# Output projection of a hybrid decoder layer: turning the normed rows three steps later, and the last weight sum behind a bank's reading

## Chip, cores and metric

The kernel runs on one core of one Trainium2 chip. The metric is the device time of one execution in microseconds (us), the median of several runs. TensorE is called PE here (PEld its weight loads), VectorE DVE, ScalarE ACT, GpSimd POOL, and SyncE, which issues most of the transfers, SP.

## What is computed

One decoder layer on a sequence of 512 rows of 1024 features in float32: a norm, an input projection, three mixing branches (dilated attention, pooling, a state space scan), gates, an output projection with the residual, then a second norm and a feed-forward part. The change lies between the output projection and the first products of the feed-forward part:

```python
merged = gates[:, :, 0] * y_a + gates[:, :, 1] * y_b + gates[:, :, 2] * y_c
x = x + merged @ w_o[i]
x = x + conv_ffn(rmsnorm(x, ln2_g[i]), ffn_w_up[i], ffn_conv_w[i], ffn_conv_b[i], ffn_w_down[i])
```

## The kernel before

Every operand of a product is split into a high part (a cast, `wh` for a weight) and a low part (the rest, `wl`), and a product is three passes: high by high, high by low, low by high. Weights come as jobs. While job n multiplies, `prepare` makes the low part of job n+1 (`low`, one DVE instruction over the tile), casts job n+2 (`cast`, two halves on ACT) and fetches job n+3. A job can have a `form`, which computes its raw weight before the cast. With `spread` the halves of a cast are put on the list `second` and issued one at each later step; with `once`, or where a job is late, they are issued at once. In `cast` the `form` is called first in either case.

The order on the engines is written out by hand: each engine executes its instructions in the order in which the program issues them. `step()` is called between blocks of products. It first flushes one entry of `second` (so one half of a cast), then advances each generator in `running` by one `yield`. `after(n, it)` puts n empty steps before a generator.

The output projection is done in seven products instead of eight (`wo_group`): two, five, three, one, six, seven, four, each with sums of weight quarters and sums of the merged rows. Each product has two blocks, one for each of two row blocks of 128 (tb 0 and 1 or 2 and 3), of 12 matmuls of 128x512. Six, seven and four add onto the banks of one, so a block must wait until the block before it on that bank has been read (`read`, DVE adds the bank to the rows `x`). The weight of four is `total(four.raw, four.raw, W[2])`, one DVE instruction over 128x2048.

After six reads a bank, the rows of tb 0 (then tb 1) are complete in both halves, and `then` norms them: `norm_late` squares them on ACT, takes the square root, and after its first `yield` computes the reciprocal, the factor `rt` and the normed rows `u` (one half on DVE, one on ACT). `norm_turn` transposes `u` on PE (8 transposes), casts the result to `uh` on ACT (2) and subtracts to `ul` on DVE (2). For tb 0 and 1 the generator `rest` was advanced once where it was made, so `u` was computed right behind the reading, and the transposes came two steps later:

```python
if tb < 2:
    r = rest()
    next(r)
    running.append(after(1, r))
```

For tb 2 and 3, which four completes, the remaining part is called from the first products of the up projection (`opening`, line 1531), which multiply the columns of tb 0 and 1 first, and those of tb 2 and 3 later. Two small transposes (`fcol`) of the convolution's constants stand among the blocks too.

Of the kernel before, what the change touches and what calls it, by code (L numbers as in the profile page):

```python
# [71 lines left out]
class Job:  # L72


    def __init__(self, parts, k, c, body):
        self.parts, self.k, self.c, self.body = parts, k, c, body
        self.raw = self.split = None
        self.late = self.short = self.once = False
        self.load = self.form = self.then = None


# [1 line left out]
def trunk(ctx: ExitStack, tc, out, x, rel_bias, ln1_g, w_in, b_gate, w_a, pool_w, pool_scale, w_b,  # L83
# [22 lines left out]
    def T(name, dt=F32, shape=(P, S)):  # L106
        return big.tile(list(shape), dt, name=name, tag="t")
# [7 lines left out]
    def small(name, shape, dt=F32):  # L115
        return tiny.tile(list(shape), dt, name=name, tag="tiny")
# [7 lines left out]
    waiting, running = [], []  # L124
# [38 lines left out]
    def after(n, it):  # L163
        for _ in range(n):
            yield
        yield from it
# [18 lines left out]
    def cast(job, cuts=1, spread=False, other=None):  # L185


        w = job.c // cuts
        if job.form:
            job.raw = job.form()  # L190
        job.high = whp.tile([P, job.k, job.c], F32R, name="wh", tag="wh")

        def high(i):
            o = slice(i * w, (i + 1) * w)
            (other.tensor_copy if other and i else act.copy)(job.high[:, :, o], job.raw[:, :, o])  # L195

        def at(i):
            high(i)
            if i + 1 < cuts:
                second.append(lambda: at(i + 1))  # L200

        if spread:
            second.append(lambda: at(0))
            return
        for i in range(cuts):
            high(i)
# [212 lines left out]
    def rstd_of(ss, cols, n):  # L419

        sq, v, r, t, r2 = (small(nme, [P, cols]) for nme in ("sq", "v", "r", "rt", "r2"))
        dve.tensor_scalar(v, ss, 1.0 / n, EPS, OP.mult, OP.add)
        act.activation(sq, v, AF.Sqrt)
        dve.reciprocal(r, sq)
        if cols == 1:
            dve.scalar_tensor_tensor(t, r, v, r, OP.mult, OP.mult)
        else:
            dve.tensor_mul(t, r, r)
            dve.tensor_mul(t, t, v)
        dve.tensor_scalar(t, t, -0.5, 1.5, OP.mult, OP.add)  # L430
        dve.tensor_mul(r2, t, r)
        return r2
# [14 lines left out]
    def norm_turn(us, uh, ul, tb):  # L447
        for h in range(2):
            ps = SM("uT")
            for j in range(4):  # L450
                pe.transpose(ps[:, j * P:(j + 1) * P], us[h][:, j * P:(j + 1) * P], eye)  # L451
            pv = ps.rearrange("p (j t) -> p j t", j=4)
            hh = uh[:, 4 * h:4 * h + 4, tb * P:(tb + 1) * P]
            act.copy(hh, pv)
            dve.tensor_sub(ul[:, 4 * h:4 * h + 4, tb * P:(tb + 1) * P], pv, hh.bitcast(F32))
# [10 lines left out]
    def norm_late(t, g, v0, outs, last, h=1, apart=False):  # L466


        ss, v, sq, r, rt = (small(n, [P, 1]) for n in ("ss", "v", "sq", "r", "rt"))
        squares(act, t, ss)  # L470
        act.activation(sq, ss, AF.Sqrt, bias=v0, scale=1.0 / D)
        xg = None
        if not apart:
            xg = T("xg")
            dve.tensor_tensor(xg, t, g[h], OP.mult)
        dve.scalar_tensor_tensor(v, ss, -0.5 / D, last, OP.mult, OP.add)
        yield xg

        dve.reciprocal(r, sq)
        dve.scalar_tensor_tensor(rt, r, v, r, OP.mult, OP.mult)  # L480
        dve.scalar_tensor_tensor(rt, rt, 1.5, r, OP.add, OP.mult)

        if apart:
            o1, (o0, x0) = outs()
            dve.scalar_tensor_tensor(o1, t, rt, g[h], OP.mult, OP.mult)
            act.mul(o0, x0, rt)
            return
        (o1, x1), (o0, x0) = outs(xg)
        act.mul(o0, x0, rt)
        dve.tensor_scalar(o1, x1, rt, None, OP.mult)  # L490
# [772 lines left out]
    def wo_group():  # L1263
# [34 lines left out]
        def then(tb, h):  # L1298
            if "uh" not in nxt:
                nxt["uh"] = upool.tile([P, KD, S], F32R, name="uh2", tag="uh")  # L1300
                nxt["ul"] = upool.tile([P, KD, S], F32R, name="ul2", tag="ul")
            v0, vh, xg0 = nxt[tb]
            us = [T("u0"), T("u1")]
            it = norm_late(X1[tb, h], nxt["g2"], v0,
                           lambda: (us[h], (us[1 - h], xg0)), vh, h, True)
            next(it)

            def rest():
                next(it, None)
                yield  # L1310
                norm_turn(us, nxt["uh"], nxt["ul"], tb)

            if tb < 2:
                r = rest()
                next(r)
                running.append(after(1, r))
            elif tb == 2:
                r2 = rest()
                next(r2)
                late.append(r2)  # L1320
            else:
                late.append(rest())
                for _ in late_split.pop(0):
                    pass
# [50 lines left out]
        def total(out, a, b, op=OP.add):  # L1375
            dve.tensor_tensor(out, a, b, op)
            return out
# [3 lines left out]
        three = job(4, None, lambda: W[1], B, (0, 1), more=True)  # L1381
        one = job("A11", quarter(0, 0), None, A, (0, 0), behind=lambda tb, h: first(tb, 1))
        six = job(2, None, lambda: W[2], A, (0, 1), more=True, op=OP.subtract, behind=then)
        seven = job(3, None, lambda: W[1], A, (1, 1), more=True, op=OP.subtract,
                    behind=lambda tb, h: first(tb, 0))
        four = job("A22", quarter(1, 0), lambda: total(four.raw, four.raw, W[2]), A, (1, 0), more=True,
                   behind=then)
        one.then = lambda: total(W[1], W[2], one.raw, OP.subtract)
        four.late, inner = True, four.body

        def body(ws):
# [209 lines left out]
    def program():  # L1601
# [21 lines left out]
        for group, next_ in zip(groups, groups[1:] + (None,)):  # L1623
# [4 lines left out]
            for i, job in enumerate(group.jobs):  # L1628
# [14 lines left out]
        many = {"a": branch_jobs(0, w_a, AO, 3), "g": gate_jobs(2),  # L1643
                "Z": z_jobs(0), "z": z_jobs(1)}
        load, sums, group = wo_group()
        for token in MIX:
            if token == "w":
# [119 lines left out]
    for tb in range(2):  # L1767
        s0, s1, v, sq, r, rt = (small(n, [P, 1]) for n in ("s0", "s1", "v", "sq", "r", "rt"))
# [13 lines left out]
    dve.tensor_copy(g1, first[2][:, :KD])  # L1782

    cast(weights[0], 2, other=dve)
    low(weights[0], 2, pool)
    for k in range(KD):
        turn_scale(1, k % 2 * 4 + k // 2)
    for k in range(KD):
        turned(k, 0, bank(k))
    cast(weights[1], 2)  # L1790
    parts = lows(weights[1], 2)

# [3 lines left out]
    r = rstd_of(ss, 2, D)  # L1796
# [25 lines left out]
    fetch(weights[3])  # L1822
    begin(0, 256, S)
    cast(weights[2])
    low(weights[2])
    begin(1, 256, S)
# [4 lines left out]
    n = 0  # L1831
# [68 lines left out]
```

## Time and profile before

| | us |
|---|---|
| median of 3 runs | 1026.0 |
| lowest, highest | 1025.07, 1026.0 |
| the profiled execution | 1025.94 |
| its span | 1024.2 |

The profile is one execution. The page gives the busy time of each engine, the chain of work that ended last, and groups of instructions by line. Answers of the trace give waits (who waited for whom), the timeline (instructions in order of time, merged where they follow each other) and windows (busy time, granted TensorE clock and DMA in stretches of the span). Times in them are counted from the start of the span. Ends of matmuls are modelled, some 0.16 us behind the next one's start, so starts are compared with starts.

### The profile page before, as it was taken

The page shows a single profiled execution, that of the slowest core. Times are in us where ns is not written, and L with a number is a line of the kernel's source. Part 1 is how long each engine was busy: PE and PEld are TensorE (multiplying, and loading weights), DVE is VectorE, ACT ScalarE, POOL GpSimd, SP SyncE. Part 2 cuts the span into 40 slices and gives each one's busy share as a digit, 9 for nine tenths or more (in the row PEclk, how much of TensorE's full clock was granted, in tenths as well). Part 3 has the DMA queues.
Part 4 walks back from the last instruction along what each step waited for, and adds up shares of the span by engine and source line. Part 5 has one row for each costly group of instructions (what it writes and reads, how often), then busy time and mean ns, then how long its engine had stood idle before and what let it go on. Part 6 is the DMA issues. An engine that isn't in the chain of part 4 may idle for free.

```text
span 1024.2 us, 13621 instructions
## 1 busy us (share of the span) xinstructions
PE 1007.2 (98%) x5378; PEld 858.4 (84%) x5378; DVE 718.8 (70%) x910; ACT 518.8 (51%) x877; POOL 141.3 (14%) x128
## 2 busy tenths in 40 slices
PE   8999999999999999999999999799999999999997
PEld 8998878999988888888888887598888888888885
DVE  6554767687757647667889687658778768685756
ACT  5433545554445476878567235554454434433434
POOL 1681000010000000000064402102111100111002
PEclk9999999999999999999999999899999999999999
DMA  8548312165254353552266255333232232321332
GB/s 255 182 110 200 108 58 79 53 155 179 90 172 107 86 134 96 143 144 83 83 166 187 91 163 149 123 110 98 86 120 83 92 114 79 128 83 42 124 103 83
DMA packets 114624, 121.26 MB, mean 118 GB/s; under 512 B 6500, under 2 KB 96167, under 8 KB 114560
## 3 DMA queue, kind: packets, MB, share of 16 engines
q1 hardware_dynamic: 111087, 114.81, 36.4%
q0 software_dynamic: 2880, 4.72, 2.8%
q8 instruction: 42, 0.69, 0.3%
q10 hardware_dynamic: 592, 0.86, 0.2%
q14 instruction: 23, 0.18, 0.1%
HBM read 116.58 MB, written 3.00 MB: 117 GB/s over the span
## 4 chain that ended last, share of the span: by engine, by line
PE 96%; DVE 2%; ACT 1%; DMA 1%; issue 0%; ACTq 0%; DVEq 0%
PE pa L236 35%; PE pu L236 22%; PE pb L236 11%; PE pd L236 7%; PE pqk L236 6%; PE pq L236 3%; PE pa L1748 2%; PE ps L784 1%; PE pu L1531 1%; PE ppw L236 1%; PE po L832 1%; PE pt L818 1%; PE py L1117 1%; DMA xin<-in_x_dram 1%; PE pyo L1124 1%; PE uT L451 0%
## 5 line engine op out<-in xcount | busy, mean ns | idle before, releaser
L215 DVE TENSOR_TENSOR wl<-raw,wh 128x2048 fp32r<-128x2048 f32 (+3 forms) x87 | 202.8, 2331 | 49.3 <-ACT wh L195 27.9
L195 ACT CAST wh<-raw 128x1024 fp32r<-128x1024 f32 (+4 forms) x171 | 171.6, 1021 | 71.4 <-DVE raw L359 17.8
L1426 DVE SCALAR_TENSOR_TENSOR hc<-pu,fcol,hc 128x510 f32<-128x510 f32 x88 | 65.9, 749 | 56.1 <-ACT hc L1423 54.5
L236 PE MATMUL pa<-uh,wh 128*128 128x512 f32 (+1 forms) x368 | 88.9, 381 | 0.0
L236 PE MATMUL pa<-ul,wh 128*128 128x512 f32 (+1 forms) x368 | 86.8, 375 | 0.0
L236 PE MATMUL pa<-uh,wl 128*128 128x512 f32 (+1 forms) x368 | 86.7, 375 | 0.0
L236 PE MATMUL pu<-uh,wh 128*128 128x512 f32 (+1 forms) x352 | 83.5, 379 | 0.0
L236 PE MATMUL pu<-ul,wh 128*128 128x512 f32 (+1 forms) x352 | 83.5, 379 | 0.0
L236 PE MATMUL pu<-uh,wl 128*128 128x512 f32 (+1 forms) x352 | 83.5, 379 | 0.0
L236 PEld LDWEIGHTS pa<-ul,wh 128*128 128x128 f32 x368 | 66.7, 188 | 12.6
L236 PEld LDWEIGHTS pa<-uh,wl 128*128 128x128 f32 x368 | 66.7, 188 | 12.5
L236 PEld LDWEIGHTS pa<-uh,wh 128*128 128x128 f32 x368 | 65.4, 189 | 11.8
L236 PEld LDWEIGHTS pu<-uh,wl 128*128 128x128 f32 x352 | 64.2, 188 | 12.5
L236 PEld LDWEIGHTS pu<-ul,wh 128*128 128x128 f32 x352 | 64.2, 188 | 12.5
L236 PEld LDWEIGHTS pu<-uh,wh 128*128 128x128 f32 x352 | 64.1, 188 | 12.4
L1423 ACT ACTIVATE hc<-pu,fcol,fcol 128x512 f32<-128x512 f32 x40 | 31.2, 779 | 78.9 <-PE pu L236 78.8
L1431 POOL TENSOR_TENSOR hc<-hc 128x512 f32<-128x512 f32 x22 | 30.8, 1399 | 284.3 <-DVE hc L1426 252.1
L215 DVE TENSOR_TENSOR wl<-w,wh 128x2048 fp32r<-128x2048 f32 (+1 forms) x22 | 47.3, 2151 | 10.2 <-issue 4.6
L806 ACT ACTIVATE sb<-sb,nmls 128x128 f32<-128x128 f32 (+1 forms) x72 | 30.0, 418 | 31.4 <-DVE nmls L803 20.8
L195 ACT CAST wh<-w 128x1024 fp32r<-128x1024 f32 (+1 forms) x44 | 41.0, 972 | 4.8 <-PE pb L236 2.4
L1100 POOL TENSOR_TENSOR st<-st,dts 128x512 f32<-128x512 f32 x4 | 4.2, 1049 | 225.9 <-ACT st L1108 163.9
L1428 ACT ACTIVATE hc<-hc 128x512 f32<-128x512 f32 x22 | 13.9, 632 | 40.2 <-DVE hc L1426 40.1
(424 smaller groups left out, 1948.8 us busy)
## 6 DMA issues: line engine op xcount, KB each, us to landing
raw<-in_w_in_dram SPq DMA_DIRECT2D x24, 1024.0 KB, 5.6
raw<-in_ffn_w_up_dram SPq DMA_DIRECT2D x22, 1024.0 KB, 5.1
raw<-in_ffn_w_down_dram SPq DMA_DIRECT2D x8, 1024.0 KB
raw<-in_w_in_dram SPq DMA_DIRECT2D x14, 512.0 KB, 5.6
raw<-in_w_in_dram SPq DMA_DIRECT2D x8, 768.0 KB
raw<-in_w_b_dram SPq DMA_DIRECT2D x4, 1024.0 KB
al<-ad SPq DMA_DIRECT2D x16, 256.0 KB, 6.2
raw<-in_w_c_dram SPq DMA_DIRECT2D x4, 1024.0 KB, 5.2
```

Of the source, the lines that this page charges most:

```text
L195: (other.tensor_copy if other and i else act.copy)(job.high[:, :, o], job.raw[:, :, o])
L215: (eng or dve).tensor_tensor(l[:, :, o], job.raw[:, :, o], h[:, :, o].bitcast(F32), OP.subtract)
L236: pe.matmul(ps, l, r, start=first and n == 0, stop=last and n == total - 1, skip_group_check=onto)
L784: pe.matmul(pss[i][:, o:o + w * P], q[r, n * P:(n + 1) * P], k[r, kb * P:(kb + w) * P], start=True, stop=True)
L806: act.activation(sb[:, off:off + w * P], sb[:, off:off + w * P], AF.Exp, bias=nm[:, n, h:h + 1], accum_out=ls[:, n, h:h + 1])
L818: pe.transpose(pt[:, o:o + P], sb[:, o:o + P], eye)
L832: pe.matmul(po[DH * hh:DH * hh + DH, n * P:(n + 1) * P], V[g, kb + i][:, (2 * c + hh) * DH:(2 * c + hh + 1) * DH], probs[2 * c + hh, nb][: ...
L1423: act.activation(t, ps, AF.Identity, bias=ff["c1"][:, ff["b"] + m:ff["b"] + m + 1], scale=fw(2, m))
L1426: dve.scalar_tensor_tensor(t[:, sh:], ps[:, :S - sh], fw(k, m), t[:, sh:], OP.mult, OP.add)
L1428: act.activation(t, t, AF.Silu)
L1431: pool.tensor_tensor(a, a, t, OP.mult)
L1748: pe.matmul(first[2 * n + j][:, lo:hi], a[:, k, j * P:(j + 1) * P], b[:, k, lo:hi], start=a is wh and b is uh and k == 0, stop=a is wl and ...
```

## The change

`rest` takes a count of empty steps, and for tb 0 and 1 it goes into `running` without being advanced: the reciprocal, the factor and `u` are computed at the next step, behind the flush of a cast, and the transposes three steps after that. Job four becomes `lazy` and six is no longer `once`: the weight sum of four and the first half of its cast are issued by the flush of the next step, behind the reading of six's first bank and the square on it, and the second half one step later.

```diff
-        self.late = self.short = self.once = False
+        self.late = self.short = self.once = self.lazy = False
...
-        if job.form:
+        if job.form and not (spread and job.lazy):
             job.raw = job.form()
...
         def at(i):
+            if i == 0 and job.lazy:
+                job.raw = job.form()
             high(i)
...
-            def rest():
+            def rest(n=1):
                 next(it, None)
-                yield
+                for _ in range(n):
+                    yield
                 norm_turn(us, nxt["uh"], nxt["ul"], tb)

             if tb < 2:
-                r = rest()
-                next(r)
-                running.append(after(1, r))
+                running.append(rest(3))
...
         one.then = lambda: total(W[1], W[2], one.raw, OP.subtract)
+        six.once, four.lazy = False, True
         four.late, inner = True, four.body
```

## The prediction

> **What bounds the kernel now.** I read the page first: the engines' busy time and the chain that ended last.
>
> ```profile
> span 1024.2 us, 13621 instructions
> ...
> PE 1007.2 (98%) x5378; PEld 858.4 (84%) x5378; DVE 718.8 (70%) x910; ACT 518.8 (51%) x877; POOL 141.3 (14%) x128
> ...
> PE 96%; DVE 2%; ACT 1%; DMA 1%; issue 0%; ACTq 0%; DVEq 0%
> ```
>
> TensorE (PE) is busy for 98% of the span and carries 96% of the chain, so a change pays only where PE stands still or runs slowly. The waits of PE over the whole span come next (waiting line, releaser, us in total, times, longest).
>
> ```profile
> PE uT L451 <- ACT u L486: 6.9, 1, 6.9
> PE uT L1765 <- DVE diag L1777: 2.0, 2, 1.7
> ```
>
> One wait stands out: 6.9 us, once, before the transposes of the normed rows, which the change moves. Windows of the span show what PE does around it (stretch, its length, PE, PEld, DVE, ACT, POOL busy, PEclk, DMA share, GB/s).
>
> ```profile
> 6.00:7.00 1.00, 0.00 (x0) 0.00 (x0) 0.85 (x4) 0.55 (x2) 0.00 (x0) 1.00 1.10 350
> 640.00:642.00 2.00, 2.00 (x11) 1.65 (x10) 2.00 (x1) 0.00 (x0) 0.15 (x1) 1.00 0.00 0
> 644.00:646.00 2.00, 0.00 (x0) 0.00 (x0) 1.10 (x2) 1.39 (x2) 0.00 (x0) 0.91 0.97 347
> 646.00:648.00 2.00, 0.00 (x0) 0.00 (x0) 0.16 (x1) 1.98 (x4) 0.00 (x0) 0.50 1.05 373
> 655.00:656.00 1.00, 1.00 (x4) 0.73 (x3) 1.00 (x2) 1.00 (x2) 0.00 (x0) 0.56 0.00 0
> 690.00:1016.00 326.00, 326.00 (x1444) 270.08 (x1444) 237.03 (x257) 141.51 (x194) 36.79 (x26) 1.00 0.29 95
> ```
>
> From 690 to 1016 PE is busy without a gap at full clock, so what is won before 690 arrives at the end, unless a later load turns late. In the wait the granted clock falls to 0.50 (a mean of 0.91 over 644 to 646 puts the fall at 645.6) and is back only near 655.9 (0.56 over 655 to 656). The timeline shows the wait link by link (start, us, engine, line, operation).
>
> ```profile
> 633.13 0.34 SPq L510 DMA_DIRECT2D fcol1r<-in_ffn_conv_b_dram  x1
> ...
> 639.83 2.47 DVE L215 TENSOR_TENSOR wl<-w,wh 128x2048 fp32r<-128x2048 f32 x1
> ...
> 641.52 1.07 PE L236 MATMUL pb<-wh,sal 128*128 128x512 f32 x4
> ...
> 642.22 2.28 DVE L1376 TENSOR_TENSOR raw<-raw,w 128x2048 f32<-128x2048 f32 x1
> ...
> 642.42 1.07 PE L236 MATMUL pb<-wl,sah 128*128 128x512 f32 x4
> 644.42 0.68 DVE L1350 TENSOR_TENSOR x<-x,pb 128x512 f32<-128x512 f32 x1
> 644.61 1.99 ACT L195 CAST wh<-raw 128x1024 fp32r<-128x1024 f32 x2 [5.07 <-DVE raw L1376]
> 646.50 0.62 ACT L437 ACTIVATE junk<-x 128x512 f32<-128x512 f32 x1
> ...
> 647.25 0.16 DVE L476 SCALAR_TENSOR_TENSOR v<-ss,vo 128x1 f32<-128x1 f32 x1 [2.16 <-ACT junk L437]
> ...
> 648.86 0.16 DVE L479 RECIPROCAL r<-sq 128x1 f32<-128x1 f32 x1 [1.45 <-ACT sq L471]
> ...
> 649.51 0.75 DVE L485 SCALAR_TENSOR_TENSOR u<-x,rt,grow 128x512 f32<-128x512 f32 x1
> 649.57 0.72 ACT L486 ACTIVATE u<-xg,rt 128x512 f32<-128x512 f32 x1 [0.74 <-DVE rt L481]
> 650.17 0.68 DVE L1350 TENSOR_TENSOR x<-x,pb 128x512 f32<-128x512 f32 x1
> ...
> 650.34 1.97 PE L451 MATMUL uT<-eye,u 128*128 128x128 f32 x8 [6.85 <-ACT u L486]
> ...
> 651.96 2.05 PE L236 MATMUL pb<-wh,sbh 128*128 128x512 f32 x4
> ...
> 652.68 0.72 ACT L486 ACTIVATE u<-xg,rt 128x512 f32<-128x512 f32 x1 [0.74 <-DVE rt L481]
> ...
> 656.62 0.27 PE L516 MATMUL fcol0p<-eye,fcol0r 128*128 128x128 f32 x1
> ...
> 657.01 1.09 PE L451 MATMUL uT<-eye,u 128*128 128x128 f32 x8
> ...
> 657.86 1.17 PE L236 MATMUL pb<-wh,sbh 128*128 128x512 f32 x4
> ```
>
> Job six has issued its last matmul at 643.3. Its first bank, done long before, is read only at 644.42, because `wl` of job seven and the weight sum of job four hold VectorE (DVE). The square on it starts at 646.50, because the cast of that sum holds ScalarE (ACT). So u is ready at 650.3, and job seven, which needs no u, stands behind the transposes.
>
> **The old cost.** From 643.3 to 650.34 are 7.0 us of no issue. Then 8 transposes, 12 matmuls of seven and no more take 650.34 to 656.62, 6.3 us. At full clock 8 transposes are 0.85 (657.01 to 657.86), 4 matmuls 0.90 (641.52 to 642.42) and so 12 are 2.7: 3.6 in all. The slow clock cost 2.7 us, the pause 7.0: 9.7 together.
>
> **The change, part by part.** The instructions are the same ones; only their places on PE, DVE and ACT move. By the instruction order of the changed program, PE goes: seven's first block, the two `fcol` transposes, seven's second block, transposes of block 0, four's first block, transposes of block 1, four's second block, then the opening of the up projection. DVE goes: `wl` of seven, first reading, v, weight sum, reciprocal to u, second reading, its chain, `wl` of four, the readings of seven. The second half of four's cast stands behind the second square root. Further durations:
>
> ```profile
> 655.11 2.28 DVE L215 TENSOR_TENSOR wl<-raw,wh 128x2048 fp32r<-128x2048 f32 x1
> ...
> 658.65 1.05 ACT L454 CAST uh<-uT 128x512 fp32r<-128x512 f32 x2
> ...
> 658.78 0.15 DVE L461 TENSOR_SCALAR v<-ss 128x1 f32<-128x1 f32 x1 [0.79 <-ACT junk L437]
> ...
> 659.35 1.28 DVE L455 TENSOR_TENSOR ul<-uT,uh 128x512 fp32r<-128x512 f32 x2
> ...
> 666.14 2.08 PE L1531 MATMUL pu<-uh,wh 128*128 128x256 f32 x16
> ...
> 668.05 2.09 PE L1531 MATMUL pu<-ul,wh 128*128 128x256 f32 x16
> ...
> 668.29 2.29 DVE L215 TENSOR_TENSOR wl<-raw,wh 128x2048 fp32r<-128x2048 f32 x1
> ...
> 679.38 1.12 PE L236 MATMUL pu<-uh,wh 128*128 128x256 f32 x8
> ```
>
> *First stall.* The first reading takes the weight sum's old start, 642.22, and ends at 642.9. Seven's first block follows six at 643.3 unstalled and issues to 646.0, the `fcol` transposes (656.62 to 657.01, 0.4) to 646.4; their data is there, for the last load was issued at 633.13 and DMA carries nothing over 640 to 642. Seven's second block adds onto the bank that the second reading empties. On DVE v comes 0.75 after the square's start (646.50 to 647.25), at 643.7; the weight sum runs 643.8 to 646.0; reciprocal to second reading is 1.31 (648.86 to 650.17), so that reading starts at 647.3 and ends at 648.0. PE waits from 646.4: 1.6 us. The square root needs 2.36 from square to reciprocal (646.50 to 648.86), to 645.3, and is covered by the sum.
>
> *Second stall.* Seven's second block and block 0's transposes (u long ready) issue to 651.6. Four's first block needs the reading of seven's first bank, which stands behind the second chain and `wl` of four. Reading to the end of u is 3.2 us (650.17 to 653.40), so `wl` starts at 650.4 and runs 2.28 to 652.7; cast halves of 1.0 fit before it (646.1 and 649.0). The reading ends at 653.3: PE waits 1.7 us.
>
> *Third stall.* Four's first block, transposes, second block: 2.7 + 0.85 + 2.7, to 659.6. The opening needs `uh` of block 1, whose casts stand on ACT behind the norm of row block 2, and that norm hangs on DVE: v and copies (658.78 to 659.35, 0.6) after the square, to 654.6; reading of seven's second bank 0.7; its square, v and the start of `ul`, 1.3, to 656.6; two `ul` 1.2, to 657.8; reading of four's first bank, whose chain ends with u at 661.0. The first of two casts (0.5 of 1.05) ends at 661.5: PE waits 1.9 us.
>
> *Fourth.* Thirty-two matmuls of 0.12 (16 in 666.14 to 668.05) and transposes issue to 666.3; the `wl` that follows ends at 666.6 (two `ul` to 662.8, reading 0.7, square and v 0.9, `wl` 2.29): 0.4 us.
>
> After that comes the old order: 16 + 32 + 16 matmuls and a set of transposes, 8.5 us from 666.6 to 675.2, against 679.3 (row 679.38; its weight load issues 0.1 ahead). In sum 9.7 less 1.6 + 1.7 + 1.9 + 0.4 is **4.1 us**. The same link lengths, set into the old order, give back 679.3.
>
> Queues: SP's second `w` load waits for the weight sum, 1.5 us later; behind it the next up-projection load waits for `wl` of four, which ends at 652.7 instead of 657.4. So weights come earlier. POOL's order is kept.
>
> *The unknown.* Does PE keep its clock through pauses of 1.6 to 1.9 us? The nearest row is the first window: at 6 to 7 us PE stood in a 1.65 us wait at clock 1.00, and the known fall came 2.1 us after the last matmul (643.5). All three pauses lie below that, and nearer the first, so I take none. The other end is one slow spell: twelve matmuls took 651.96 to 656.62, 4.7 instead of 2.7, so 2.0 us. The Trainium skill, "TensorE: Matmul & The Clock Gate", section "What's actually happening", puts the fall after an idle window of about 3.4 us of a free-running counter. By that no pause here would slow PE, and the sum stays 4.1; the trace's fall after 2.1 us speaks for a shorter one.
>
> **The rivals.** *One slow spell.* Block 0's transposes and the second stall together are 2.6 us without a product, more than 2.1. If transposes do not hold the clock, four's first block runs at half, costing up to 2.0, of which some 0.8 hides in the third stall's DVE chain; a fall in the third stall costs 1.5. Gain 2.1 to 2.9, so about 1023.4. For it: recovery at 655.9 came 5.5 us after the transposes began but 3.9 after the products; against it: only one event. The same page, Part 4, says that transposes do not count as PE activity; its result would be this rival's.
>
> *The clock never recovers: slower.* Recovery took 5.5 us of unbroken issue; the new stalls lie 3.6 and 6 us apart. If the first stall drops the clock and every further one restarts the count, PE runs at half from 648 to 668: 10 us of work in 20, where the forecast does 16 (20 less 4 of stalls). That costs 6: 1.9 us slower than now, 1027.9. It decides from a slow stretch of some 14 us on. Against it: the 1.65 us pause at full clock.
>
> *Nothing left.* DVE now sets three PE restarts in a row. If hand-overs between ACT and DVE each take longer than in the old order, by 2 us over the chain of some 15 links, the gain falls under 0.2%: 1024.5 to 1026. Against it: the link lengths reproduce the old timeline.
>
> **How the numbers follow.** The profiled execution took 1025.94 (span 1024.2 and 1.7 around it); the median is 1026.0, so I subtract from that: 1026.0 − 4.1 = 1021.9, own range 1020.4 to 1023. Chances: forecast 0.62, one spell 0.2, nothing left 0.11, slower 0.07. About 0.2%, 2.05 us, is what measurement can tell: faster below 1023.95. That is the forecast and most of the spell (0.18): 0.8; within 0.13; slower 0.07. The range 1020.4 to 1024.8 takes in the spell at its dearest (1021.9 + 2.0) and part of the third rival.
>
> **What would show it.** Right: PE's 6.9 us wait gone, in its place waits of about 1.6, 1.7 and 1.9 us on `x` L1350 or its line, and on `uh`; full clock over 640 to 670; the opening at 661.5 instead of 666.1; the tail matmuls at 675.2 instead of 679.4. Wrong: a clock of 0.50 anywhere from 646 to 668, a stall above 2.5 us, a wait after 690, or the tail later than 677.

## The result, and the profile after

| | before | after |
|---|---|---|
| median of 7 runs each, us | 1025.58 | 1021.8 |
| lowest, highest, us | 1024.67, 1026.0 | 1021.59, 1022.39 |
| the profiled execution, us | 1025.94 | 1021.8 |
| its span, us | 1024.2 | 1020.0 |

The ratio of the times is 0.9967, 95% interval 0.9955 to 0.9979: faster, by 4.1 us in the profiled executions and 3.8 between the medians, where 4.1 was forecast.

The waits of PE in the changed kernel (waiting line, releaser, us in total, times, longest; lines stand one or two lower than before):

```profile
PE pb L238 <- DVE x L1351: 3.0, 2, 1.5
PE pu L1533 <- ACT uh L456: 1.5, 1, 1.5
...
PE pb L238 <- DVE wl L217: 0.2, 1, 0.2
```

The wait of 6.9 us on `u` is gone; two waits on the readings of banks and one on `uh` stand in its place. The timeline of PE says where they are (start, us, operation, in brackets the idle time before and its releaser):

```profile
642.46 1.07 PE L238 MATMUL pb<-wl,sah 128*128 128x512 f32 x4
...
648.04 1.21 PE L238 MATMUL pb<-wh,sbh 128*128 128x512 f32 x4 [1.49 <-DVE x L1351]
...
650.94 1.03 PE L453 MATMUL uT<-eye,u 128*128 128x128 f32 x8
653.45 1.17 PE L238 MATMUL pb<-wh,mgh 128*128 128x512 f32 x4 [1.47 <-DVE x L1351]
...
661.56 2.18 PE L1533 MATMUL pu<-uh,wh 128*128 128x256 f32 x16 [1.49 <-ACT uh L456]
...
665.50 1.03 PE L453 MATMUL uT<-eye,u 128*128 128x128 f32 x8
666.63 2.18 PE L1533 MATMUL pu<-uh,wl 128*128 128x256 f32 x16
...
675.26 1.12 PE L238 MATMUL pu<-uh,wh 128*128 128x256 f32 x8
```

From the last matmul group of job six (row 642.46, before 642.42) to the first group of the tail (675.26, before 679.38) PE needs 32.80 us instead of 36.96: 4.16 less, the whole gain. On DVE and SP the same stretch shows the links that set these starts:

```profile
642.25 0.68 DVE L1351 TENSOR_TENSOR x<-x,pb 128x512 f32<-128x512 f32 x1
643.72 0.16 DVE L478 SCALAR_TENSOR_TENSOR v<-ss,vo 128x1 f32<-128x1 f32 x1 [0.79 <-ACT junk L439]
643.80 2.29 DVE L1377 TENSOR_TENSOR raw<-raw,w 128x2048 f32<-128x2048 f32 x1
646.00 0.16 DVE L481 RECIPROCAL r<-sq 128x1 f32<-128x1 f32 x1
...
647.31 0.68 DVE L1351 TENSOR_TENSOR x<-x,pb 128x512 f32<-128x512 f32 x1
...
650.42 2.28 DVE L217 TENSOR_TENSOR wl<-raw,wh 128x2048 fp32r<-128x2048 f32 x1
652.63 0.68 DVE L1351 TENSOR_TENSOR x<-x,pb 128x512 f32<-128x512 f32 x1
652.74 0.37 SPq L182 DMA_DIRECT2D raw<-in_ffn_w_up_dram  x1
```

The reading takes the place of the weight sum, the reciprocal follows the sum without a gap (the square root is covered), and the next load of weights is issued at 652.74. Windows (stretch, length, busy time of PE, PEld, DVE, ACT, POOL, granted clock, DMA share, GB/s):

```profile
647.00:648.00 1.00, 0.00 (x0) 0.00 (x0) 0.99 (x2) 0.84 (x2) 0.00 (x0) 1.00 0.37 80
652.00:653.00 1.00, 0.00 (x0) 0.00 (x0) 1.00 (x2) 0.52 (x1) 0.00 (x0) 1.00 0.00 0
660.00:661.00 1.00, 0.07 (x1) 0.00 (x0) 0.93 (x3) 0.69 (x2) 0.00 (x0) 1.00 0.00 0
686.00:1011.80 325.80, 325.80 (x1442) 270.01 (x1442) 236.97 (x256) 141.38 (x194) 36.80 (x26) 1.00 0.29 95
```

In the windows with the waits the clock stays at 1.00, and behind the stretch PE is busy without a gap again. Nothing was given back.

### The profile page after: what moved, and what is told of

It is laid out like the page before. It is cut to its first block, busy times and chain, and to the rows that moved or that the text cites. A ratio compares the mean times of both kernels' runs of the same rounds, so it can differ in the third digit from the quotient of the medians.

```text
span 1020.0 us, 13623 instructions
## 1 busy us (share of the span) xinstructions
PE 1006.3 (99%) x5378; PEld 857.5 (84%) x5378; DVE 719.4 (71%) x910; ACT 518.3 (51%) x877; POOL 143.8 (14%) x128
## 4 chain that ended last, share of the span: by engine, by line
PE 95%; DVE 3%; ACT 1%; DMA 1%; issue 0%; ACTq 0%; DVEq 0%
PE pa L238 36%; PE pu L238 22%; PE pb L238 9%; PE pd L238 7%; PE pqk L238 6%; PE pq L238 3%; PE pa L1750 2%; PE ps L786 1%; PE ppw L238 1%; PE po L834 1%; DVE wl L217 1%; PE pt L820 1%; PE py L1119 1%; PE pu L1533 1%; DMA xin<-in_x_dram 1%; ACT junk L439 1%
## 5 line engine op out<-in xcount | busy, mean ns | idle before, releaser
L217 DVE TENSOR_TENSOR wl<-w,wh 128x2048 fp32r<-128x2048 f32 (+1 forms) x22 | 47.3, 2149 | 10.2 <-issue 4.6
```

Source lines behind the costliest of these rows:

```text
L217: (eng or dve).tensor_tensor(l[:, :, o], job.raw[:, :, o], h[:, :, o].bitcast(F32), OP.subtract)
```

## The experiments

Whole times of the same kernel differ between executions, by 0.8 us over the seven of the changed kernel. In its two profiles the difference (0.3 us) lies ahead of this stretch: six's last group starts at 642.46 and 642.75, and an early wait of PE, on `diag`, totals 1.0 us in the first and 2.1 in the second. So the kernels are compared by **the stretch**: from the start of six's last matmul group to the first group of the tail, in the profiled execution. It is one execution of each kernel. Where not said otherwise an edit is against the changed kernel.

| kernel | stretch, us | median, us | ratio to before, 95% interval |
|---|---|---|---|
| before | 36.96 | 1025.58 | |
| changed | 32.80 | 1021.8 | 0.9967 (0.9955 to 0.9979) |
| `after_again` | 32.80 | 1022.81 | 0.997 (0.9959 to 0.9982) |
| `turn_only` | 35.72 | 1025.5 | 0.9995 (0.9986 to 1.0004) |
| `sum_only` | 35.46 | 1025.52 | 0.9994 (0.9985 to 1.0003) |
| `warm_pause` | 35.51 | 1025.42 | 0.9994 (0.9985 to 1.0002) |
| `late_read1` | 33.68 | 1023.08 | 0.9966 (0.9956 to 0.9977) |
| `late_read3` | 34.84 | 1024.88 | 0.9991 (0.9981 to 1.0) |
| `read_first` | 34.08 | 1023.08 | 0.997 (0.9959 to 0.9982) |
| `both_turn` | 31.89 | 1021.93 | 0.996 (0.9946 to 0.9974) |
| `both_pool` | 32.61 | 1022.25 | 0.9966 (0.9954 to 0.9979) |

The medians were taken in four groups of runs, so they can't be compared down the whole column: the kernel before had 1025.58 beside the changed kernel, 1026.27 beside `turn_only`, `sum_only` and `warm_pause`, 1026.59 beside the two `late_read` kernels and 1025.92 beside the others. The intervals of the first three include 1: their gains are seen in the stretch alone.

The changed kernel run again (`after_again`) gave the stretch to 0.01 us.

> The changed kernel itself, for a comparison on this chip: 0.9967 of before, 3.4 us (4.1 by its profile).

**The turning alone** (`turn_only`).

```diff
-        six.once, four.lazy = False, True
```

> Only the turning is moved; the weight sum of job four and both halves of its cast stay ahead of the first reading of six. Theory (the order on VectorE and ScalarE sets when PE may go on, and the two parts pay fully only together): the first reading stays at 644.4, so seven's first block waits 1.8 us for it, its second block 2.6 us for the second reading at 650.9, then 1.7, 1.9 and 0.4 as in the changed kernel; the first of the tail's 128x256 matmuls at 678.1 to 678.2 instead of 679.4, and the time 1.2 us under before, some 1024.4 to 1024.9. Rival (the transposes ahead of seven were the wait, the weight sum a small extra): most of the 4.1 us comes from here, 3 us or more.

It measured 35.72, 1.24 less than before. Timeline of PE:

```profile
646.07 1.15 PE L238 MATMUL pb<-wh,sbh 128*128 128x512 f32 x4 [1.75 <-DVE x L1351]
...
651.75 2.07 PE L238 MATMUL pb<-wh,sbh 128*128 128x512 f32 x4 [2.41 <-DVE x L1351]
...
665.26 2.19 PE L1532 MATMUL pu<-uh,wh 128*128 128x256 f32 x16 [1.59 <-ACT uh L456]
```

Job seven no longer waits for `u`, but the weight sum and both halves of the cast are still ahead of the reading and the square. The first two waits are 1.75 and 2.41, and in the second the clock falls (four matmuls take 2.07), which was not expected. The wait of 1.7 expected ahead of four's first block did not come; the slow spell took its place, and the opening waits for `uh` all the same. So the total agrees (1.2 expected), though not its parts.

**The weight sum alone** (`sum_only`): the edits to `cast` and the line of `six` and `four`, on the kernel before, with its turning.

```diff
+            if i == 0 and job.lazy:
+                job.raw = job.form()
...
+        six.once, four.lazy = False, True
```

> Only the weight sum and its cast are moved; the transposes stay ahead of job seven. Theory: PE's wait ahead of the transposes falls from 6.9 to 3.3 us, but what comes next hangs on the ScalarE and VectorE chain: the tail's 128x256 matmuls start at 677.9 to 678.0 instead of 679.4, 1.4 us under before, whether the clock falls in the wait or not (a slow clock then only fills later waits). Rival: the 3.5 us by which the wait shortens arrive whole, and with them part of the 2.7 us of slow clock: 3.5 us or more under before.

It measured 35.46, 1.50 less. Timeline of PE:

```profile
647.65 1.97 PE L453 MATMUL uT<-eye,u 128*128 128x128 f32 x8 [3.28 <-ACT u L488]
...
655.51 1.25 PE L453 MATMUL uT<-eye,u 128*128 128x128 f32 x8 [1.06 <-DVE ul L457]
```

`u` comes earlier (a wait of 3.28 instead of 6.85), but seven still stands behind the transposes, and the clock falls. Alone the parts give 1.24 and 1.50, and both at once 4.16: each removes one of two things that kept PE waiting at the same place.

**The pause without the slow clock** (`warm_pause`): the kernel before with 28 idle matmuls on PE, whose results are overwritten, ahead of block 0's transposes.

```diff
+            if tb == 0 and h == 0 and uh is nxt.get("uh"):
+                for _ in range(28):
+                    pe.matmul(ps, ones, MH[1][0], start=True, stop=True)
```

> The kernel before with 28 matmuls of 128x512 whose result is overwritten, put into the pause of PE ahead of the transposes of row block 0; nothing else changes. They keep PE busy for 6.35 of the 7.0 us. Theory: the granted clock stays at 1.00 through 643 to 660, but of the 2.7 us of slow clock only about 1.4 us arrive, because the transposes of row block 1 and what follows then wait for VectorE (0.4, 0.2, 0.2 and 0.6 us). Rival, by the prediction's own account (pause 7.0 and slow clock 2.7 add up): 2.7 us under before. If the clock falls all the same: no change.

The first view is the timeline of PE, the second a window over the stretch:

```profile
644.26 6.71 PE L452 MATMUL uT<-mgh,ones 128*128 128x512 f32 x28
651.28 1.09 PE L454 MATMUL uT<-eye,u 128*128 128x128 f32 x8 [0.30 <-ACT u L489]
...
656.60 1.17 PE L236 MATMUL pb<-wh,sbh 128*128 128x512 f32 x4
```

```profile
644.00:668.00 24.00, 23.54 (x121) 19.08 (x120) 15.18 (x35) 14.58 (x28) 2.59 (x2) 1.00 0.39 132
```

The transposes start 7.92 us after six's last group, as before, and the clock is 1.00 throughout, but the stretch is 1.45 shorter and not 2.7. From the transposes to seven's second block it takes 5.32 instead of 7.52: 2.2 saved, the other 0.5 went to new waits, for `ul` among them. From there to the tail it takes 22.27 instead of 21.52, since PE now arrives before the low weights: 0.75 given back.

**One and three more DVE operations ahead of the reading of seven's first bank** (`late_read1`, n = 1, and `late_read3`, n = 3; the sums go to a tile that nothing reads).

```diff
+                    if j == 3 and i == 0:
+                        for _ in range(n):
+                            dve.tensor_tensor(T("idle"), X1[2, 0], X1[2, 0], OP.add)
```

> The changed kernel with one idle DVE addition (128x512, 0.68 us, its result unused) ahead of the reading of job seven's first bank, so that PE's second wait grows from 1.5 to 2.1 us. The kernels with one part alone, and the one before, showed the clock falling 2.1 to 2.3 us after the last matmul and not in a wait of 1.75. Theory: no fall, or one at the very edge; 0.7 us over the changed kernel, the tail's first 128x256 matmul 33.4 to 33.5 us after the start of the last matmul group of six (32.8 in the changed kernel). Rival (transposes don't hold the clock: they stand ahead of this wait, so 3.0 us pass without a product): it falls, and 1.8 us over the changed kernel.

> The same with three idle additions: the wait grows to 3.5 us. Theory: the clock falls 2.1 to 2.3 us into it, stays at 0.50 for some 3.4 to 5.5 us, and 2.0 us of delay plus 1.1 of slow clock make 3.1 us over the changed kernel (the tail 35.9 us after the last group of six). If only a wholly idle stretch of 3.4 us dropped it, no fall in most executions and 2.0 us over the changed kernel (34.8).

They measured 33.68 and 34.84, 0.88 and 2.04 over the changed kernel. Timelines of PE, `late_read1` first:

```profile
656.76 1.46 PE L238 MATMUL pb<-wh,mgh 128*128 128x512 f32 x4 [2.08 <-DVE x L1354]
...
665.13 2.18 PE L1536 MATMUL pu<-uh,wh 128*128 128x256 f32 x16 [0.15 <-ACT uh L456]
```

```profile
656.02 1.17 PE L238 MATMUL pb<-wh,mgh 128*128 128x512 f32 x4 [3.28 <-DVE x L1354]
657.03 1.82 PE L238 MATMUL pb<-wh,mgl 128*128 128x512 f32 x4
...
664.36 2.18 PE L1536 MATMUL pu<-uh,wh 128*128 128x256 f32 x16
```

In both the clock falls, but only after PE has started again (in `late_read3` the first four matmuls after the wait take 1.17, the next four 1.82), and for 3.4 us, which costs 1.7. The third wait nearly disappears, for the DVE chain behind `uh` runs while PE is slow. `late_read3`: second wait +1.81, clock +1.7, third wait −1.49, in sum 2.02. `late_read1`: +0.61 + 1.7 − 1.34 = 0.97. The full price of a fall on top of the slip (3.1 for three) did not come; 2.04 is the size that was expected without a fall, though the clock did fall here.

The fall in `late_read1` is not its usual course. A spell of 3.4 us at half clock takes 0.0017 off the mean granted clock of the span, and six of its eight executions have 0.999, which leaves no room for one. The profiled execution has 0.995 and was the longest (1025.41 against a median of 1023.08): besides the spell shown it had one at 12.32 to 15.73, behind the early waits on `diag`. So "no fall, or one at the very edge" was right for most executions; whether these were 0.7 over the changed kernel is not shown.

**The second reading ahead of the reciprocal** (`read_first`).

```diff
-                running.append(rest(3))
+                running.append(after(1, rest(2)))
```

> The changed kernel with u of row blocks 0 and 1 computed one step later still, so that the second reading of six stands ahead of the first block's reciprocal and u on DVE. Theory: the first wait falls from 1.6 to 0.3 us, but the time comes back behind it: u of row block 1 is late, its uh is late, and the wait ahead of the up projection grows from 1.9 to 3.2 us (over 2.1, so the clock may fall there, at 1.5 us); with a fall 1.7 us over the changed kernel, without it 0.2 over. Rival (each wait is its own, and what is saved at one arrives): 1.3 us under the changed kernel.

It measured 34.08 in the profiled execution, 1.28 over the changed kernel. Timeline of PE:

```profile
647.52 1.20 PE L238 MATMUL pb<-wh,sbh 128*128 128x512 f32 x4 [0.18 <-DVE x L1351]
...
662.50 3.05 PE L1533 MATMUL pu<-uh,wh 128*128 128x256 f32 x16 [2.85 <-ACT uh L456]
```

The first wait goes (0.18), and 1.36 of it is back in the third (2.85), for block 1's norm now stands behind `wl` of four on DVE; there the clock falls. The median is only 0.27 above that of `after_again`, and one of the six executions had a mean clock of 0.999, so here too the fall does not come in every execution.

**Both sets of transposes together** (`both_turn`), ahead of four's two blocks, and the `fcol` transposes three steps later.

```diff
-                running.append(rest(3))
+                running.append(rest(3 - tb))
...
-            yield
-            yield
+            for _ in range(5):
+                yield
```

> The changed kernel with the transposes of row block 1 one step earlier, right behind those of block 0 and so inside the second wait, and the two small fcol transposes three steps later, which frees their banks. Theory: the second wait falls from 1.7 to 0.9 us, the wait ahead of the up projection from 1.9 to 0, the first one grows by the 0.4 us of the fcol transposes to 1.9, and the wait for wl of the up projection grows from 0.4 to 1.9; in sum 1.0 us under the changed kernel, 0.9957 to 0.9960 of before. Rival (the chain on DVE and ACT sets the end whatever the place of the transposes): the same time as the changed kernel.

It measured 31.89, 0.91 less than the changed kernel. Timeline of PE:

```profile
649.06 1.32 PE L238 MATMUL pb<-wh,sbh 128*128 128x512 f32 x4 [1.80 <-DVE x L1351]
...
653.50 1.91 PE L453 MATMUL uT<-eye,u 128*128 128x128 f32 x16
...
666.73 2.17 PE L1533 MATMUL pu<-uh,wl 128*128 128x256 f32 x16 [0.65 <-DVE wl L217]
```

The second and third wait are gone. The first, now without the `fcol` transposes ahead of it, is 1.80, and in this execution the clock falls for 3.4 us. The total is near the 1.0 us that was expected, but not by the expected parts: the second wait (0.9) did not come and the wait for `wl` of the up projection is 0.65 and not 1.9, for the slow spell, which was not expected, used up that time. On the same chip `after_again` had a median of 1022.81 and this kernel 1021.93; the intervals of their ratios overlap, so the stretch says that it is the better one, the whole time alone does not.

**The weight sum on GpSimd as well** (`both_pool`, against `both_turn`).

```diff
-            dve.tensor_tensor(out, a, b, op)
+            eng.tensor_tensor(out, a, b, op)
...
-        six.once, four.lazy = False, True
+        six.once = False
```

The call for four passes `eng=pool`.

> As both_turn, and the weight sum of job four is done by GpSimd, issued in job six's preparation, instead of by DVE. GpSimd takes 1.29 us for 128x512, so about 5.2 us for this one, from 640.2 to 645.4. Theory: DVE is free of 2.28 us, but the square root and the table load ahead of it hold the chain, so only 0.7 us arrive: 1.6 us under the changed kernel. Rival (DVE and GpSimd slow each other): nothing, or worse than both_turn.

It measured 32.61, 0.72 more than `both_turn`. The timelines of GpSimd (first row) and DVE:

```profile
641.28 6.66 POOL L1377 TENSOR_TENSOR raw<-raw,w 128x2048 f32<-128x2048 f32 x1
...
643.40 0.68 DVE L1351 TENSOR_TENSOR x<-x,pb 128x512 f32<-128x512 f32 x1
644.86 3.09 DVE L478 SCALAR_TENSOR_TENSOR v<-ss,vo 128x1 f32<-128x1 f32 x1 [0.79 <-ACT junk L439]
```

The sum takes 6.66 us there, and DVE's `v`, an operation on 128x1 that takes 0.16 elsewhere (row 643.72 above), takes 3.09 and ends at 647.95, with GpSimd's (647.94). What was taken off DVE came back as a blocked DVE: the rival's outcome, and not the 1.6 us that was expected.

## Why the prediction was right, and where a step was off

**The links of DVE and ACT: right.** Forecast starts against the rows above:

| | forecast | measured |
|---|---|---|
| first reading of six | 642.22 | 642.25 |
| second reading of six | 647.3 | 647.31 |
| seven's second block | 648.0 | 648.04 |
| `wl` of four | 650.4 | 650.42 |
| four's first block | 653.3 | 653.45 |
| opening | 661.5 | 661.56 |
| third group of the opening | 666.6 | 666.63 |
| tail | 675.2 | 675.26 |

No start is off by more than 0.15 us. The instructions keep their durations, so following the new order on each engine, hand-over by hand-over, was enough. "Nothing left", where each link was to become longer, is refuted. The waits read 1.49, 1.47 and 1.49 instead of 1.6, 1.7 and 1.9, because the trace counts them from modelled ends of matmuls and the forecast from issue to issue. Counted from the end of issue, by the spacing of starts, they are 1.57, 1.72 and 1.65: the third was put 0.25 too long, since four's first block began 0.15 late, and four's two blocks and the transposes took 0.2 more than the summed 6.25. For the weight loads, which issue first, the waits read as forecast (waits of PEld, after; the one ahead of four's first block is listed under its cast):

```profile
PEld pu L1533 <- ACT uh L456: 1.9, 1, 1.9
...
PEld pb L238 <- ACT wh L195: 1.7, 1, 1.7
PEld pb L238 <- DVE x L1351: 1.6, 1, 1.6
```

**The sum: right as an account, wrong as a list of prices.** Within one kernel the time of the stretch is work, waits, and half of the time that PE works at half clock; `turn_only` against the changed kernel is waits of 5.75 instead of 4.45 and a spell of 3.4 us at half clock, 1.3 + 1.7 = 3.0, measured 2.92. But "the slow clock cost 2.7 us, the pause 7.0" reads as if each could be had by itself. Taking only the slow clock away brought 1.45, half of that term, and the two halves of the change brought 1.24 and 1.50 out of 4.16. PE stands under a chain of DVE and ACT that runs by its own time: a cause that goes hands its place to the next one. The forecast came out because it worked out what is late next at each restart.

**The clock: the outcome right, the reading wrong.** The prediction read a limit of 2.1 us after the last matmul. In `late_read3` the clock was still full then and fell 1.1 us after PE had resumed; in `both_turn` a wait of 1.80, below that limit, ended in a fall. That no pause of the change crossed the real limit was therefore in part luck. A count over fixed stretches of 3.41 us fits all kernels here: counted backwards from the moment of the fall (worked out from windows of 1 us), PE's busy time in one such stretch was (row of windows: length, then PE busy; before, `turn_only`, `both_turn`, `late_read3`):

```profile
642.24:645.65 3.41, 1.25 (x6) 0.71 (x4) 2.86 (x3) 1.04 (x2) 0.00 (x0) 1.00 0.54 181
```

```profile
644.78:648.19 3.41, 2.12 (x9) 1.80 (x10) 1.24 (x3) 2.73 (x5) 0.00 (x0) 1.00 0.97 314
648.19:651.60 3.41, 1.15 (x6) 0.65 (x4) 1.86 (x6) 2.19 (x3) 0.00 (x0) 1.00 0.72 262
```

```profile
646.57:649.98 3.41, 1.61 (x8) 1.02 (x7) 2.48 (x7) 2.58 (x5) 0.00 (x0) 1.00 0.88 286
649.98:653.39 3.41, 3.41 (x10) 2.62 (x9) 3.17 (x5) 3.41 (x5) 0.00 (x0) 0.50 0.44 171
```

```profile
646.88:650.30 3.42, 1.92 (x9) 1.37 (x8) 2.31 (x8) 3.15 (x6) 0.00 (x0) 1.00 0.75 259
...
653.71:657.12 3.41, 1.10 (x5) 0.95 (x6) 2.58 (x7) 0.73 (x2) 1.11 (x1) 1.00 0.75 152
```

The stretches shown with 1.10 to 1.61 us of work end in a fall, as do those of the other kernels, with 0.97 to 1.34; those with 1.92 and 2.12 (the first rows of `late_read3` and `turn_only`, on the same grid) do not.

The early part of the span narrows this: the early spell of `late_read1` follows a stretch with 1.71 us of work (8.91 to 12.32), while 1.76 in the kernel before (3.93 to 7.34) and 1.80 in `both_turn` (8.27 to 11.68) kept the clock. That the stretches are fixed is seen in the traces' records of the clock: from its first rise, 4 to 6.5 us into the span, to the fall in the stretch there are 188 times 3.4133 us in the kernel before and `sum_only`, 189 in `turn_only`, `both_turn` and `both_pool`, 191 in the `late_read` kernels and 193 in `read_first`. So where a wait lies on this grid, which differs between executions, decides too: 1.75 us in `turn_only` left 2.12 us of work in its stretch and did not lower the clock.

The longest wait of the changed kernel is 1.49 and its waits lie further apart than 3.41, so between 640 and 680 no stretch of 3.41 us, wherever it begins, has less than 1.92 us of work: by this count that is why its clock stays up, in both profiled executions. One of its 13 executions (1024.66 us, mean clock 0.996) must have had a spell; without a trace of it, where is not known.

The Trainium skill, "TensorE: Matmul & The Clock Gate", section "What's actually happening", gives a free-running window of 3413 ns, and the length agrees: in the stretch six spells of 3.4 us, one of 6.8 (`sum_only`), one of 10.2 (before). It asks for an idle window before a fall; here windows with 47% and 50% of work (1.61 and 1.71 of 3.41) were enough, and the measurement decides. The limit between 1.71 and 1.76 is read from one execution of each kernel, with modelled ends of matmuls, and no run was made to find it alone; it stays a fit.

**The rivals.** "One slow spell" did not occur, though the profiled execution of `late_read1` had one at that place; it cost 0.88 there, the slip included, not 1.2 to 2.0, because more of it hides in the third wait (1.34) than the 0.8 allowed. "The clock never recovers" is refuted for such stalls: in the six kernels in which PE was at work within 0.2 us of the fall, the spell ended after one window. The condition of the first rival, that transposes do not hold the clock, had no run of its own, but two kept traces speak against it: stretches on their grids with 0.96 us of products (matmuls that are no transposes) in `read_first` (649.81 to 653.22) and 1.05 in `sum_only` (653.32 to 656.73), 2.06 and 2.36 with the transposes, kept full clock, while `both_turn` fell with 1.61 us of products and no transposes.

## What to carry over

Read a stall as a queue of causes: at each restart of the bound engine write down who is late next, and add up restarts, not causes. A cause tried by itself can be worth half of what it seems, and two that meet at one wait more together than their sum. Where PE must wait, keep waits short and far apart: three of 1.5 us kept the full clock, one of 1.8 lost it for 3.4 us in the profiled execution of `both_turn`. And look at what DVE does before moving work to GpSimd: here the sum moved there held up a DVE operation with two inputs from SBUF, and nothing was gained.

## What had not been expected of the hardware

- The clock can fall after PE is back at work, for work that was missing earlier in the window: 1.1 us after it resumed in `late_read3`.
- GpSimd's sum over 128x2048 took 6.66 us, where four of its sums over 128x512 at 1.30 make 5.2, and a DVE operation of 0.16 us beside it took 3.09, until GpSimd had ended. The Trainium skill, "SBUF — State Buffer", section "Who interferes with whom", says that a DVE instruction with two inputs from SBUF contends with a GpSimd instruction that reads SBUF. That agrees: `v` reads `ss` and `vo`, while DVE's reading of a bank at 643.40, with one input from PSUM, took its usual 0.68 during the same sum. The first 2.2 us of the sum lie beside DVE's `wl` of seven (641.00 to 643.48, two inputs from SBUF); whether GpSimd waited there, which would leave 4.46 of the 6.66, is not shown.
